# Eight weights of a token-major product prepared ahead, and the MLP's rings in groups of four neighbouring buffers

## The chip, the cores and the metric

The kernel runs on one core of a Trainium2 chip. Its time is the device time of one execution in microseconds (us), lower is better. TensorE (PE) multiplies matrices, with its weight loads shown apart as PEld; VectorE is DVE, ScalarE is ACT, GpSimd is POOL, and SyncE (SP) issues the transfers. Before the change three runs gave 3012.39, 3013.59 and 3018.19 us, a median of 3013.59 us.

## The reference

Two layers, each of three sub-layers on 1024 tokens of width 1024, with a layer norm after each. All is in float32.

```python
def hybrid_mixer(x, positions, w_in, conv_w, rel_bias, w_out):
    proj = jnp.einsum('bsd,dp->bsp', x, w_in)
    (cb, cc, ch, dq, dk, dv, iq, ik, iw, cq, ck, cv) = jnp.split(proj, offs, axis=-1)
    y_conv = short_conv_mixer(cb, cc, ch, conv_w)
    ...                      # partial rope on dq, dk, iq, ik
    y_dsa = dsa_attention(dq, dk, dv, iq, ik, iw)
    y_chk = chunk_band_attention(cq, ck, cv, rel_bias)
    return jnp.einsum('bsm,md->bsd', jnp.concatenate([y_conv, y_dsa, y_chk], -1), w_out)
...
        # in dsa_attention, for each block of 128 queries
        score = jnp.einsum('bqh,bqhs->bqs', iwb, jax.nn.relu(logits))
        _, idx = lax.top_k(score, topk)            # topk = 256
        s = ...                                    # attention on the chosen keys alone
...
for l in range(DEPTH):                             # DEPTH = 2
    x = layer_norm(ALPHA * x + hybrid_mixer(...))
    x = layer_norm(ALPHA * x + memory_cross_attention(x, mem, w_mq, w_mkv, w_mo))
    x = layer_norm(ALPHA * x + squared_relu_mlp(x, w_ff1, w_ff2))   # 1024 -> 4096 -> 1024
```

## The kernel before

Every large product keeps float32 accuracy with rounded operands: an operand is split into a rounded part `hi` and the rest `lo`, and `mm3` (L338) adds three matmuls, hi·hi (L340), hi·lo (L341) and lo·hi (L342). A weight passes through `Weights._emit` (L274): SP moves it to one of four stage buffers (L284), ACT casts it to `hi` (L285), POOL subtracts to get `lo` (L286). `Weights.get(i)` does this for weights up to i + AHEAD, with AHEAD = 4, before the product that uses weight i is written; `prefetch(i)` does it up to weight i where there is room. Both write the instructions at that place in the program. The Tile framework then orders the instructions of each engine by priority and by a simulated timeline, and the engines run their lists in that order. An `Arena` hands out SBUF columns by which of them came free longest ago; a buffer that is taken again makes its new writer wait for the old readers.

Each layer begins with the input projection. Three groups are token-major, by `tok_tile` (L550): the indexer's (key `g1`, weights 128x296), the DSA queries, keys and values (`dsa_proj`, `g2`, 128x512) and the chunk attention's values (`chk_v`, `g3`, 128x384). A group has eight weights, used by all of its eight token tiles, and the first tile of a group asks for its weights one by one with `get`. The chunk queries and keys and the convolution's inputs follow, feature-major. Beside the projections the indexer computes `queries` (L690: rope, a split on POOL L699, a transpose on PE L708), scores each of eight heads on PE (L731), applies the relu on ACT (L736) and sums on DVE (L742 and L744). `topk` (L761) then finds each query's threshold bit by bit, 32 bits: blocks 7 and 6 (group 0) are counted on ACT with Sign (L788), blocks 5 to 2 (group 1) on DVE (L792), and L799 to L811 update the candidate. `masks` (L820) turns thresholds into masks. POOL and DVE also apply the rope (L440 to L443), and L644 (ACT) with L645 (DVE or POOL) is the split of an activation.

`chunk_pair` (L1010) prepares the operands of the chunk attention: ACT scales and rounds the queries (L1022), DVE subtracts (L1023), SP moves halves between partitions (L1019, rows "sb<-sb"); ACT rounds the keys (L1036), POOL subtracts (L1037), and SP moves again. The first scores on PE (L1088) use them. Chunk units and then DSA units follow with their softmax, the weights of the memory products are worked on beside them, and then come the mix output product, the cross attention and its output product.

The MLP is a Strassen product at one level. `up` takes seven products for each of 16 chunks and writes the results `h` to DRAM; the down half takes steps `(p, i)`, p in 5, 7, 3, 1, 4, 6, 2 and i of 16, each of four token tiles with 3 matmuls. `prepare(n)` (L1798) loads an `h` tile and a weight into two `raws` buffers, adds the parts of the weight, and splits both into a `pairs` buffer; DOWN_AHEAD = 7 steps are ahead. `raws` is a ring of 8 buffers of 512 columns, `slots` a ring of kept weights; both are allocated one by one between the two halves.

## Time and profile before

| what | value |
|---|---|
| median of three runs | 3013.59 us |
| profiled execution, its own time | 3010.65 us |
| its span | 3008.8 us |
| PE busy | 2884.2 us, 96% of the span, 14440 matmuls |
| DVE busy | 2155.3 us, 72% |
| ACT busy | 1558.0 us, 52% |
| POOL busy | 1299.5 us, 43% |
| mean DMA rate | 127 GB/s |

The span is that of the one profiled execution, whose own time is 1.85 us longer. PE is the engine that is busy nearly all the time, so the idle time of PE, and the stretches in which PE ran at the lower of its two clock levels, are what can be removed or added without a change of work. In a timeline row the figures are the start, the length of the group of equal instructions, the instruction, and in brackets the idle time of the engine before it with the engine and line that ended it.

### The profile page before, as it was taken

The numbers are of one execution on the slowest core, as the hardware profiler recorded it, in microseconds if no ns is written. First come the engines' busy times: TensorE is split into PE (matmuls) and PEld (weight loads), VectorE is DVE, ScalarE is ACT, GpSimd is POOL, SyncE is SP. The second block draws the span as 40 slices with busy tenths as digits, with TensorE's granted clock in tenths as the row PEclk, the third lists the DMA queues.
The fourth block names the chain that finished last, engine by engine and source line by source line (L and its number), as shares of the span: only waits on it lengthen the run. The fifth ranks groups of instructions, "written<-read, shape, count | busy, mean of one in ns | idle before, by whom it ended". The sixth has DMA issues, their size and how long they took to land. (4 is left out here: it accounts for less than half of the span.)

```text
span 3008.8 us, 43448 instructions
## 1 busy us (share of the span) xinstructions
PE 2884.2 (96%) x14440; PEld 2440.8 (81%) x14440; DVE 2155.3 (72%) x4321; ACT 1558.0 (52%) x3146; POOL 1299.5 (43%) x1242
## 2 busy tenths in 40 slices
PE   8999889999999999999999998899999999999998
PEld 7787778788877788888788877887888778888886
DVE  5897786582487766777857987866625877667788
ACT  5676777623234455543457767784222445554432
POOL 4614575522335553222457146653222555532223
PEclk9999999999999999999999999999999999999999
DMA  4213333331334546755422144232213354476553
GB/s 127 63 36 85 101 110 106 105 119 36 114 116 161 171 154 217 255 178 188 131 68 66 37 100 118 92 117 97 93 47 111 112 175 163 152 250 223 189 179 116
DMA packets 264288, 381.99 MB, mean 127 GB/s; under 512 B 23040, under 2 KB 141824, under 8 KB 264064
## 3 DMA queue, kind: packets, MB, share of 16 engines
q1 hardware_dynamic: 264064, 379.22, 38.7%
q8 instruction: 114, 1.87, 0.3%
q14 instruction: 110, 0.90, 0.1%
HBM read 269.56 MB, written 95.42 MB: 121 GB/s over the span
## 5 line engine op out<-in xcount | busy, mean ns | idle before, releaser
L340 PE MATMUL banks<-sb,sb 128*128 128x512 f32 (+3 forms) x3776 | 1423.0, 378 | 19.7 <-DVE sb L645 6.3
L341 PE MATMUL banks<-sb,sb 128*128 128x512 f32 (+3 forms) x3776 | 1417.7, 376 | 8.6 <-POOL sb L286 8.6
L342 PE MATMUL banks<-sb,sb 128*128 128x512 f32 (+3 forms) x3776 | 1413.9, 376 | 7.7 <-POOL sb L645 7.4
L645 POOL TENSOR_TENSOR sb<-sb,sb 128x512 fp32r<-128x512 f32 (+1 forms) x428 | 590.1, 1390 | 931.3 <-ACT sb L644 793.5
L340 PEld LDWEIGHTS banks<-sb,sb 128*128 128x128 f32 x3776 | 714.3, 189 | 151.4 <-DVE sb L645 9.1
L342 PEld LDWEIGHTS banks<-sb,sb 128*128 128x128 f32 x3776 | 712.7, 189 | 133.2 <-POOL sb L645 9.2
L341 PEld LDWEIGHTS banks<-sb,sb 128*128 128x128 f32 x3776 | 714.4, 189 | 130.8 <-POOL sb L286 10.3
L644 ACT CAST sb<-sb 128x512 fp32r<-128x512 f32 (+1 forms) x788 | 452.8, 605 | 583.5 <-PE banks L341 146.2
L286 POOL TENSOR_TENSOR sb<-sb,sb 128x512 fp32r<-128x512 f32 (+2 forms) x288 | 381.4, 1340 | 480.1 <-ACT sb L285 421.2
L645 DVE TENSOR_TENSOR sb<-sb,sb 128x512 fp32r<-128x512 f32 x360 | 273.2, 785 | 43.8 <-ACT sb L644 41.4
L645 DVE TENSOR_TENSOR sb<-banks,sb 128x384 fp32r<-128x384 f32 (+2 forms) x324 | 188.0, 595 | 86.4 <-ACT sb L644 78.9
L285 ACT CAST sb<-sb 128x512 fp32r<-128x512 f32 (+2 forms) x288 | 170.4, 606 | 136.1 <-PE banks L342 30.4
L644 ACT CAST sb<-banks 128x384 fp32r<-128x384 f32 (+2 forms) x324 | 159.7, 517 | 140.5 <-PE banks L1557 75.3
L792 DVE TENSOR_SCALAR_CACHE_REDUCE sb<-sb,sb 128x768 bf16<-128x768 f32 (+3 forms) x256 | 207.5, 810 | 5.0 <-POOL sb L443 2.0
L1721 DVE TENSOR_TENSOR sb<-sb,sb 128x512 f32<-128x512 f32 x160 | 155.5, 1006 | 60.9 <-ACT sb L1701 56.9
L1005 POOL TENSOR_SCALAR sb<-sb,sb 128x128 f32<-128x128 f32 (+7 forms) x192 | 148.2, 786 | 86.4 <-DVE sb L1003 65.9
L1763 DVE TENSOR_TENSOR sb<-banks,sb 128x512 f32<-128x512 f32 x224 | 149.4, 682 | 47.4 <-PE banks L342 45.7
L788 ACT ACTIVATE sb<-sb,sb 128x1024 bf16<-128x1024 f32 (+1 forms) x128 | 140.4, 1097 | 74.2 <-DVE sb L811 64.9
L1826 DVE TENSOR_TENSOR sb<-sb,sb 128x512 f32<-128x512 f32 x128 | 112.8, 882 | 68.4 <-DMA sb<-w_ff_dram 68.0
L994 ACT ACTIVATE sb<-sb,sb 128x128 f32<-128x128 f32 (+7 forms) x192 | 141.6, 739 | 27.9 <-DVE sb L988 26.5
L1700 ACT ACTIVATE sb<-sb 128x512 f32<-128x512 f32 x128 | 80.7, 631 | 117.6 <-DVE sb L1763 117.1
L1333 DVE SCALAR_TENSOR_TENSOR sb<-sb,banks 128x512 f32<-128x512 f32 x64 | 43.4, 685 | 113.2 <-PE banks L342 110.5
(172 smaller groups left out, 3046.9 us busy)
## 6 DMA issues: line engine op xcount, KB each, us to landing
sb<-h SPq DMA_DIRECT2D x236, 256.0 KB, 3.1
h<-sb SPq DMA_DIRECT2D x224, 256.0 KB, 2.2
sb<-w_ff_dram SPq DMA_DIRECT2D x216, 256.0 KB, 3.1
sb<-w_ff_dram SPq DMA_DIRECT2D x64, 512.0 KB, 4.1
sb<-w_in_dram SPq DMA_DIRECT2D x64, 256.0 KB, 2.9
sb<-w_mkv_dram SPq DMA_DIRECT2D x64, 256.0 KB, 2.8
sb<-sb SPq DMA_DIRECT2D x54, 256.0 KB, 3.6
xs<-sb SPq DMA_DIRECT2D x24, 512.0 KB, 2.8
```

Source lines behind the costliest of these rows:

```text
L285: k.nc.scalar.copy(hi, st)
L286: k.nc.gpsimd.tensor_tensor(lo, st, hi.bitcast(F32), op=ALU.subtract)
L340: mm(out, lh, rh, start=start, stop=False)
L341: mm(out, lh, rl, start=False, stop=False)
L342: mm(out, ll, rh, start=False, stop=stop)
L644: nc.scalar.copy(hi, src)
L645: eng.tensor_tensor(lo, src, hi.bitcast(F32), op=ALU.subtract)
L792: nc.vector.tensor_scalar(junkb[:, :w], x, c, None, op0=ALU.is_ge, op1=ALU.add, accum_out=n)
L994: nc.scalar.activation(pt.ap, pt.ap, AF.Exp, bias=mn, scale=-1.0, accum_out=sm)
L1005: nc.gpsimd.tensor_scalar(pt.ap, pt.ap, rc[:, i : i + 1], 0.0, op0=ALU.mult, op1=ALU.add)
L1721: nc.vector.tensor_tensor(z.ap, x, y, op=ALU.add if spec[1] == "+" else ALU.subtract)
L1763: nc.vector.tensor_tensor(r.ap, ps.ap, part[c, x].ap, op=ALU.add)
```

## The change

Three edits. First, `tok_tile` ends with a `prefetch`: after the tiles t = 4, 5, 6, 7 of a group it asks for the weights up to 2, 4, 6 and 8 behind the group's last one. Since `get` has by then prepared four behind it, the tiles 4 and 5 write nothing new; weights 5 and 6 of the next group are now written behind tile 6, weights 7 and 8 behind tile 7, where they were written in the first tile of the next group. Second, `carve` is built on a new `try_carve`, and the DSA output buffer `st["ys"]` falls back to three buffers where no room for one is left; the number of instructions in the built program shows that the fallback is not taken (32 of the joint add, as before). Third, the MLP takes five groups of four neighbouring 512-column buffers at the top of the arena; the eight `raws` and the first twelve new `slots` come from them.

```diff
     def tok_tile(self, xt, key, l, t, n, last):
...
             if last:
                 self.w.done(wi[k])
+
+        if t >= NT - 4:
+            self.w.prefetch(wi[-1] + 2 * (t - NT + 5))
         return ps
...
-    def carve(self, *cols):
+    def try_carve(self, *cols):
...
-        b = self.alloc(sum(g) * GRAN, top=True)
+        b = self.try_alloc(sum(g) * GRAN, top=True)
+        if b is None:
+            return None
...
-                parts = sb.carve(S, S, S)
-                y = st["ys"] = sb.tensor(parts[0].off, 3 * S, F32)
+                one = sb.try_carve(S, S, S)
+                parts = one or [sb.alloc(S, top=True) for _ in range(3)]
+                st["ys"] = sb.tensor(parts[0].off, 3 * S, F32) if one else None
...
         self.up(l, ops, weights, combos, pend, early())
         ready(0)
         first = len(have)
+
+        fours = [b for _ in range(5) for b in sb.carve(512, 512, 512, 512)]
...
-        raws += [sb.alloc(512) for _ in range(8)]
-        slots += [kept[i] for i in range(first)]
-        slots += [sb.alloc(512) for _ in range(nk + 2 - first)]
+        raws += fours[:8]
+        slots += [kept[i] for i in range(first)] + fours[8:]
+        slots += [sb.alloc(512) for _ in range(nk + 2 - len(slots))]
```

No instruction is added or removed on any engine, but the lists are ordered anew. In the changed kernel the lines are numbered higher: L286 becomes L293, L440 to L443 become L447 to L450, and from L645 on 10 are added (L655, L754, L802, L1032, L1046).

On POOL, in layer 0, the end of the preparation of the `g3` weights (128x384), with the rope of a token tile and the first 128x512 weights of the products that follow. Before:

```order
L286 TENSOR_TENSOR sb_652<-sb_107,sb_652 128x512
L442 TENSOR_TENSOR sb_1047<-sb_1262,sb_794 128x6x8
L443 TENSOR_TENSOR sb_1047<-sb_1262,sb_794 128x6x8
L442 TENSOR_TENSOR sb_1260<-sb_1057,sb_1267 128x8
L443 TENSOR_TENSOR sb_1260<-sb_1057,sb_1267 128x8
L645 TENSOR_TENSOR sb_620<-sb_1260,sb_620 128x64
L286 TENSOR_TENSOR sb_324<-sb_97,sb_324 128x512
L286 TENSOR_TENSOR sb_659<-sb_112,sb_659 128x512
L286 TENSOR_TENSOR sb_1306<-sb_102,sb_1306 128x384
L645 TENSOR_TENSOR sb_577<-sb_1260,sb_577 128x64
```

and now:

```order
L449 TENSOR_TENSOR sb_735<-sb_964,sb_1203 128x6x8
L450 TENSOR_TENSOR sb_735<-sb_964,sb_1203 128x6x8
L449 TENSOR_TENSOR sb_710<-sb_970,sb_1208 128x8
L450 TENSOR_TENSOR sb_710<-sb_970,sb_1208 128x8
L293 TENSOR_TENSOR sb_1264<-sb_107,sb_1264 128x384
L655 TENSOR_TENSOR sb_731<-sb_710,sb_731 128x64
L293 TENSOR_TENSOR sb_310<-sb_97,sb_310 128x512
L293 TENSOR_TENSOR sb_317<-sb_102,sb_317 128x512
L655 TENSOR_TENSOR sb_725<-sb_710,sb_725 128x64
L293 TENSOR_TENSOR sb_1268<-sb_112,sb_1268 128x384
L293 TENSOR_TENSOR sb_324<-sb_107,sb_324 128x512
```

The last 384-wide subtract stood behind three 512-wide ones (before the first of which the other 384-wide ones stand), and now behind two, with the seventh 384-wide one directly ahead of them.

On ACT, in layer 1, the end of the search (Sign, L788, now L798) and the first rounded keys of the chunk attention (the cast L1036, now L1046). Before:

```order
L943 COPY sb_79<-banks 128x512
L788 ACTIVATE sb_901,sb_13627<-sb_12496,sb_13627 128x896
L788 ACTIVATE sb_901,sb_13627<-sb_12498,sb_13627 128x1024
L968 COPY sb_6719<-banks 128x512
L788 ACTIVATE sb_901,sb_13627<-sb_12496,sb_13627 128x896
L644 CAST sb_2817<-sb_3231 128x8x64
L788 ACTIVATE sb_901,sb_13627<-sb_12498,sb_13627 128x1024
L1036 CAST sb_2629<-sb_2748 128x1024
L788 ACTIVATE sb_901,sb_13627<-sb_12496,sb_13627 128x896
L968 COPY sb_905<-banks 128x512
L285 CAST sb_2823<-sb_112 128x512
L644 CAST sb_2825<-sb_3231 128x8x64
```

and now, from the rounded queries (L1032) on:

```order
L1032 ACTIVATE sb_2615<-sb_8191 128x1024
L798 ACTIVATE sb_845,sb_13605<-sb_12496,sb_13605 128x1024
L798 ACTIVATE sb_845,sb_13605<-sb_12494,sb_13605 128x896
L654 CAST sb_2816<-sb_3693 128x8x64
L978 COPY sb_841<-banks 128x512
L1046 CAST sb_2812<-sb_1674 128x1024
L798 ACTIVATE sb_845,sb_13605<-sb_12496,sb_13605 128x1024
L292 CAST sb_1007<-sb_112 128x512
L798 ACTIVATE sb_845,sb_13605<-sb_12494,sb_13605 128x896
L978 COPY sb_837<-banks 128x512
L654 CAST sb_1834<-sb_3693 128x8x64
L798 ACTIVATE sb_845,sb_13605<-sb_12496,sb_13605 128x1024
```

The first cast of the keys had one Sign of the search left behind it in its list, and now has four; the rounded queries had ten behind them and now have six.

On DVE, in layer 1, the sum of the scores (L744, now L754; 128x896 is block 6) and the first counts of the search's group 1 (L792, now L802). Before:

```order
L742 TENSOR_SCALAR sb_12496<-sb_13376,sb_340 128x896
L744 SCALAR_TENSOR_TENSOR sb_12496<-sb_3735,sb_340,sb_12496 128x896
L744 SCALAR_TENSOR_TENSOR sb_12496<-sb_1291,sb_340,sb_12496 128x896
L744 SCALAR_TENSOR_TENSOR sb_12496<-sb_1227,sb_340,sb_12496 128x896
L744 SCALAR_TENSOR_TENSOR sb_12496<-sb_1286,sb_340,sb_12496 128x896
L792 TENSOR_SCALAR sb_4486,sb_13627<-sb_12494,sb_13627 128x768
L744 SCALAR_TENSOR_TENSOR sb_12496<-sb_13443,sb_340,sb_12496 128x896
L792 TENSOR_SCALAR sb_4486,sb_13627<-sb_12492,sb_13627 128x640
L744 SCALAR_TENSOR_TENSOR sb_12496<-sb_5154,sb_340,sb_12496 128x896
L792 TENSOR_SCALAR sb_4486,sb_13627<-sb_12490,sb_13627 128x512
L744 SCALAR_TENSOR_TENSOR sb_12496<-sb_13452,sb_340,sb_12496 128x896
L742 TENSOR_SCALAR sb_12498<-sb_135,sb_340 128x1024
```

and now:

```order
L754 SCALAR_TENSOR_TENSOR sb_12492<-sb_3459,sb_340,sb_12492 128x768
L752 TENSOR_SCALAR sb_12494<-sb_1227,sb_340 128x896
L802 TENSOR_SCALAR sb_899,sb_13605<-sb_12492,sb_13605 128x768
L802 TENSOR_SCALAR sb_899,sb_13605<-sb_12490,sb_13605 128x640
L802 TENSOR_SCALAR sb_899,sb_13605<-sb_12488,sb_13605 128x512
L754 SCALAR_TENSOR_TENSOR sb_12494<-sb_13366,sb_340,sb_12494 128x896
L802 TENSOR_SCALAR sb_899,sb_13605<-sb_12486,sb_13605 128x384
L814 TENSOR_SCALAR sb_13605<-sb_13605 128x4
L819 TENSOR_SCALAR sb_13605<-sb_13605 128x4
L802 TENSOR_SCALAR sb_899,sb_13605<-sb_12492,sb_13605 128x768
L754 SCALAR_TENSOR_TENSOR sb_12494<-sb_3739,sb_340,sb_12494 128x896
L802 TENSOR_SCALAR sb_899,sb_13605<-sb_12490,sb_13605 128x640
```

The first counts stood behind four of the 896-wide sums, between further sums, and now stand ahead of all but the first instruction of that block.

## Rows read from the trace of the kernel before

**Rows 1.** Page of the profile: span, then busy time and instructions of each engine.

```profile
span 3008.8 us, 43448 instructions
...
PE 2884.2 (96%) x14440; PEld 2440.8 (81%) x14440; DVE 2155.3 (72%) x4321; ACT 1558.0 (52%) x3146; POOL 1299.5 (43%) x1242
```

**Rows 2.** Windows: start and end, length, busy time by engine, clock, DMA share, GB/s.

```profile
113.00:155.00 42.00, 37.79 (x193) 33.86 (x192) 41.56 (x71) 26.46 (x55) 19.61 (x25) 0.96 0.34 89
...
126.30:129.70 3.40, 3.14 (x10) 2.33 (x9) 3.40 (x6) 1.52 (x3) 0.51 (x2) 0.50 0.50 128
...
1050.00:1425.00 375.00, 375.00 (x1657) 310.59 (x1655) 271.17 (x374) 182.83 (x315) 130.94 (x93) 1.00 0.58 199
...
1590.00:1613.00 23.00, 23.00 (x117) 20.12 (x116) 11.42 (x11) 16.14 (x34) 17.60 (x33) 1.00 0.14 40
...
2525.00:2925.00 400.00, 400.00 (x1766) 331.21 (x1765) 292.95 (x404) 195.56 (x337) 141.63 (x100) 1.00 0.58 197
```

**Rows 3.** Waits of PE, one kind: total us, times, longest.

```profile
PE banks L341 <- POOL sb L286: 8.6, 4, 2.5
```

**Rows 4.** PE's timeline, layer 0: start, length, instruction, idle before and releaser.

```profile
106.86 0.88 PE L708 MATMUL banks<-sb,sb 128*128 128x128 f32 x8 [1.28 <-POOL sb L699]
...
125.59 0.45 PE L341 MATMUL banks<-sb,sb 128*128 128x384 f32 x1 [2.54 <-POOL sb L286]
...
296.17 6.72 PE L1088 MATMUL banks<-sb,sb 128*128 128x128 f32 x18 [4.89 <-DMA sb<-sb]
```

**Rows 5.** PE's timeline, layer 1.

```profile
1615.00 0.44 PE L341 MATMUL banks<-sb,sb 128*128 128x384 f32 x1 [1.59 <-POOL sb L286]
...
1618.90 0.45 PE L341 MATMUL banks<-sb,sb 128*128 128x384 f32 x1 [2.19 <-POOL sb L286]
...
1785.06 3.61 PE L1088 MATMUL banks<-sb,sb 128*128 128x128 f32 x10 [2.21 <-DMA sb<-sb]
```

**Rows 6.** POOL's timeline, layer 0 and layer 1.

```profile
121.25 4.29 POOL L286 TENSOR_TENSOR sb<-sb,sb 128x512 fp32r<-128x512 f32 x3
...
1604.37 1.02 POOL L286 TENSOR_TENSOR sb<-sb,sb 128x384 fp32r<-128x384 f32 x1
...
1613.94 4.90 POOL L286 TENSOR_TENSOR sb<-sb,sb 128x384 fp32r<-128x384 f32 x3
```

**Rows 7.** ACT's timeline, end of the search, layer 0 and layer 1.

```profile
280.93 1.15 ACT L788 ACTIVATE sb<-sb,sb 128x1024 bf16<-128x1024 f32 x1 [0.61 <-DVE sb L811]
...
282.08 1.04 ACT L1022 ACTIVATE sb<-sb 128x1024 fp32r<-128x1024 f32 x1
...
285.04 1.05 ACT L1036 CAST sb<-sb 128x1024 fp32r<-128x1024 f32 x1
...
1751.63 1.06 ACT L1022 ACTIVATE sb<-sb 128x1024 fp32r<-128x1024 f32 x1
...
1773.11 1.04 ACT L1036 CAST sb<-sb 128x1024 fp32r<-128x1024 f32 x1
```

**Rows 8.** VectorE's timeline, the search in layer 0 and layer 1.

```profile
106.19 1.10 DVE L742 TENSOR_SCALAR sb<-sb,sb 128x896 f32<-128x896 f32 x1 [1.35 <-ACT sb L736]
...
115.83 1.16 DVE L744 SCALAR_TENSOR_TENSOR sb<-sb,sb,sb 128x896 f32<-128x896 f32 x1
...
121.23 2.25 DVE L744 SCALAR_TENSOR_TENSOR sb<-sb,sb,sb 128x896 f32<-128x896 f32 x1
...
1645.27 0.15 DVE L811 SCALAR_TENSOR_TENSOR sb<-sb 128x2 int32<-128x2 int32 x1
...
1649.11 0.15 DVE L811 SCALAR_TENSOR_TENSOR sb<-sb 128x2 int32<-128x2 int32 x1
```

**Rows 9.** Page of the profile: two groups of instructions (busy us, mean ns), one DMA issue.

```profile
L645 POOL TENSOR_TENSOR sb<-sb,sb 128x512 fp32r<-128x512 f32 (+1 forms) x428 | 590.1, 1390 | 931.3 <-ACT sb L644 793.5
...
L644 ACT CAST sb<-sb 128x512 fp32r<-128x512 f32 (+1 forms) x788 | 452.8, 605 | 583.5 <-PE banks L341 146.2
...
sb<-h SPq DMA_DIRECT2D x236, 256.0 KB, 3.1
```

More of the change, by code (lines that the diff above doesn't have):

```diff
@@ L161, in carve @@
         return res
+    def carve(self, *cols):
+        b = self.try_carve(*cols)
+        assert b is not None, ("SBUF is full", cols, self.room())
+        return b
     def room(self):
@@ L1258, in values @@
             if b == 0 and hg == 0:
-                parts = sb.carve(S, S, S)
-                y = st["ys"] = sb.tensor(parts[0].off, 3 * S, F32)
+                one = sb.try_carve(S, S, S)
+                parts = one or [sb.alloc(S, top=True) for _ in range(3)]
+                st["ys"] = sb.tensor(parts[0].off, 3 * S, F32) if one else None
                 for f, x in enumerate(parts):
-                    st["y"][2 + f] = Part(x, y[:, f * S : (f + 1) * S])
-            y = st["ys"]
-            nc.vector.tensor_tensor(
-                y.rearrange("p (f s) -> p f s", f=3)[
-                    hg * HD : (hg + 1) * HD, :, b * P : (b + 1) * P
-                ],
-                po.ap[0:HD, 0:384].rearrange("p (f s) -> p f s", f=3),
-                low.ap[0:HD, :].rearrange("p (f s) -> p f s", f=3), op=ALU.add,
-            )
+                    y = st["ys"][:, f * S : (f + 1) * S] if one else x.ap
+                    st["y"][2 + f] = Part(x, y)
+            rows, q = slice(hg * HD, (hg + 1) * HD), slice(b * P, (b + 1) * P)
+            if st["ys"] is not None:
+                nc.vector.tensor_tensor(
+                    st["ys"].rearrange("p (f s) -> p f s", f=3)[rows, :, q],
+                    po.ap[0:HD, 0:384].rearrange("p (f s) -> p f s", f=3),
+                    low.ap[0:HD, :].rearrange("p (f s) -> p f s", f=3), op=ALU.add,
+                )
+            else:
+                for f in range(3):
+                    c = slice(f * P, (f + 1) * P)
+                    nc.vector.tensor_tensor(
+                        st["y"][2 + f].ap[rows, q], po.ap[0:HD, c], low.ap[0:HD, c],
+                        op=ALU.add,
+                    )
             self.ps.free(po)
```

## The prediction

> **What bounds the kernel now.** I read the page first. PE is busy 2884.2 of 3008.8 us [rows 1], so no other engine bounds the kernel as a whole, and an edit that adds and removes no instruction can only move three things: PE's idle time (3008.8 - 2884.2 = 124.6 us), the stretches at PE's lower clock level, and what ends PE's waits. Next I took the windows by stage. In both MLPs PE is busy 375.00 of 375 and 400.00 of 400 us at a granted clock of 1.00 [rows 2]: nothing is to be gained there, and what matters is how much room stands before PE starts to wait. Third, the table of PE's waits by kind shows what the change aims at, the third product of a token tile waiting for the weight's `lo` part from POOL: 8.6 us in 4 waits [rows 3]. Fourth, PE's timeline shows where. One of the waits is in layer 0 (2.54 us at 125.59), two are in layer 1 (1.59 at 1615.00, 2.19 at 1618.90) [rows 4, 5], together 6.3 us; the fourth, 8.6 - 6.3 = 2.3 us, is in another product that the change doesn't touch. Last I followed both layers to the point where the projections give way to the first chunk scores. There PE waits for the moves between partitions, 4.89 us at 296.17 and 2.21 us at 1785.06 [rows 4, 5]. That is the important thing to see: a stall that is removed earlier in the same layer brings PE sooner to a wait that a different chain ends, that of the search on ACT and DVE, the operands behind it, and their moves.
>
> **The edits that cost nothing.** The new `carve` and its fallback issue the same instructions. The MLP's rings lie elsewhere, so a load may wait for the last reader of other columns; the first four `raws` now lie where an operand of the second-last up product was. The cover is PE's queue. A matmul takes 375.00/1657 = 0.226 us there [rows 2]; the up product still to run after that one has 12 matmuls (2.7 us), and the first four steps of the down half, prepared earlier, have 4 x 12 (10.9 us), together 13.6 us. A step prepared in a new buffer needs a load of 3.1 us, a cast of 0.605 and a split of 1.39, and the cast and split again for the second operand at most, 3.1 + 2 x 2.0 = 7.1 us [rows 9]. So the rings cost 0, and if the cover were gone it would be up to 7.1 us once per layer.
>
> **The prefetch in layer 0.** It can remove the wait at 125.59: 2.54 us, and with it the low clock that follows. From 126.3 to 129.7 PE was busy 3.14 us at a granted clock of 0.50 (1.2 GHz), after the engine had stood still; at the full level the same work takes half, 1.6 us less [rows 2, 4]. That makes 4.1 us for PE. How sure is it? In the order the last 384-wide subtract on POOL still stands behind two 512-wide ones, where it stood behind three; three subtracts together took 4.29 us [rows 6], so it may come about 1.4 us sooner, besides what the earlier load gives. The bounds of the stall itself are 0 and 4.1.
>
> How much of it reaches the first scores is set by the other chain. Their operands move as follows: in the new list of ACT the rounded queries (L1022) stand one Sign earlier, ahead of that at 280.93, which began after 0.61 us of waiting and took 1.15 [rows 7]. So they, and the moves behind them, may come 0.61 + 1.15 = 1.76 us earlier at the same pace of the search. The search itself may begin earlier: at 106.86 PE waits 1.28 us for the queries' split on POOL, and just before, at 106.19, DVE had stood still 1.35 us for the relu [rows 4, 8]; in POOL's new list this split stands ahead of a rope. I count 1.0 of the 1.28. Layer 0 so gives 1.8 + 1.0 = 2.8 us; its bounds are 0 and 4.1 + 1.3 = 5.4.
>
> The subtracts are moved beside the dense part of the search, and there they have a price. DVE is busy 41.56 of 42 us from 113 to 155 [rows 2], so whatever slows it there moves the search as a whole. A sum of block 6 took 1.16 us at 115.83 and 2.25 us at 121.23, where POOL's three subtracts ran [rows 6, 8]. They ran in the dense part before, too, so I count no new cost. The Trainium skill ("SBUF — State Buffer", section "Who interferes with whom") says that DVE and GpSimd share one pair of ports under an exclusive lock; by this rule two more subtracts there would take from DVE up to 2 x (2.25 - 1.16) = 2.2 us, and layer 0 would give 2.8 - 2.2 = 0.6 instead of 2.8. The trace agrees that a sum beside the subtracts is slower, 2.25 against 1.16 us, and not that the whole of it is new.
>
> **The prefetch in layer 1.** The two stalls are 1.59 + 2.19, and a third of 0.5 us follows them in the same place, together 4.3 us at the full clock. POOL made three 384-wide subtracts in 4.90 us there, where one alone took 1.02 [rows 6]: its late `lo` parts are partly DVE's doing. Against this stands the other chain, which now runs in another order. First gain: the first cast of the keys stands behind 60 Signs, not 63 (before, at 1773.11 [rows 7]), so its operands can come earlier than 1773.11 at an equal pace. First loss: the rounded queries stand behind 58, not 54 (before, at 1751.63), yet 1751.63 lies far ahead of the keys and sets nothing. The pace is the open term. The scores' products of the last block come later in the new program, and group 1's search ends with four bits of group 0 left, not two. Near the end of group 1 a bit takes 1649.11 - 1645.27 = 3.84 us [rows 8]. If group 1's search starts no earlier, the end of group 0 comes two bits later, 7.7 us. It can start earlier: its first counts stand ahead of the 896-wide sums now, and from 1590 to 1613 DVE is busy only 11.42 of 23 us, 11.6 us idle [rows 2]. So layer 1 lies between -7.7 and +4.3. I take 2.5, nearer to the upper end, because the idle 11.6 us are more than the 7.7 that they must cover, and less than 4.3, because PE's 2.21 us of waiting at 1785.06 shows that the operands are late already.
>
> **The attention units** are ordered anew in both layers, with no instruction more or less. Some of PE's 124.6 idle us lie there, behind splits and softmax steps on DVE, and a new order can lose or gain; no row says which, so I count 0. As the nearest measure for both ends I take the waits of rows 4 and 5 that are not on weights, 4.89 + 2.21 + 1.28 = 8.4 us [rows 4, 5].
>
> **The sum.** 2.8 + 2.5 = 5.3 us, against the profiled execution 3010.65 - 5.3 = 3005.3. The median of the runs stands 2.9 us above that execution, so in medians 3013.6 - 5.3 = 3008.3, which I give as 3008.
>
> **The rivals.** A difference of 0.2%, 6 us, is about what a measurement of this kernel can tell from none.
>
> A, the forecast, 3008, chance 0.50. Its own range is 3013.6 - 9.7 = 3004 (both layers at their upper bound, 5.4 + 4.3) to 3011 (half of the sum), and it is faster by over 0.2% in about half of these cases: 0.24 faster, 0.25 same, 0.01 slower.
>
> B, absorbed: PE comes earlier to the first scores and waits longer there, or POOL's last subtract of `g3`, still behind two wide ones, is hardly sooner. For it speaks the 4.89 us wait at 296.17, larger than all that is removed before it; against it that the operands, too, stand earlier in ACT's lists of both layers. What is left is the 1.0 of the queries' split: 3012.6. Chance 0.17: 0.02, 0.13, 0.02.
>
> C, slower: in layer 1 the search starts no earlier and ends two bits later, so masks and the DSA scores behind them come 7.7 us later, and the counts and Signs run on into the attention, where they stand ahead of the softmax on DVE and ACT. It decides if group 1's first count does not come at least 7.7 us sooner than the sums allow now. The price is 7.7: 3021. For it speaks that three subtracts and the rope stand beside DVE there, and that the last block's score products come later in the new lists; against it the 11.6 idle us before. Chance 0.18: 0, 0.01, 0.17.
>
> D, faster: the stalls go, and the new order of the attention units also takes out some 6 to 7 of the waits there, 5.3 + 6.7 = 12, or 3001.6, say 3001. For it speaks that these waits are short and follow single late splits; against it that nothing in the edits aims at them. Chance 0.15, all faster.
>
> Together: faster 0.24 + 0.02 + 0.15 = 0.41, same 0.25 + 0.13 + 0.01 = 0.39, slower 0.01 + 0.02 + 0.17 = 0.20. The range reaches from 2996, where the upper bounds of both layers meet an attention better by 8, to 3021, where C stands.
>
> **What the profile afterwards would show.** The first step is right if no wait of L341 (now L348) for POOL's subtract is left near 125 and 1615, and if the clock is 1.00 after 126. The second is right if PE waits at the first chunk scores no longer than 4.89 + (5.4 - 2.8) = 7.5 and 2.21 + (4.3 - 2.5) = 4.0 us; if these grow by all that went before, it is B. Rival C shows as a last Sign of layer 1 that ends later against the end of the projections, with the first counts no earlier. The MLP windows must still show PE busy all the time; a wait of the products for a load of `h` would make the zero for the rings wrong. The prediction as a whole is wrong if the difference lies outside of the attention and projection stages.

## The result and the profile after

The changed kernel is slower. Four runs gave 3026.74 to 3032.12 us, median 3029.9; the ratio to the kernel before (now four runs, median 3013.8) is 1.0057 [1.0045, 1.0069], 0.6% or some 17 us. Its profiled execution took 3026.74 us (span 3025.0), 16.2 us of span more than the one of before.

The page, for [rows 1] (span; busy time by engine):

```profile
span 3025.0 us, 43421 instructions
...
PE 2895.5 (96%) x14440; PEld 2449.3 (81%) x14440; DVE 2161.7 (71%) x4321; ACT 1558.4 (52%) x3146; POOL 1292.2 (43%) x1242
```

PE is busy 11.3 us longer with the same 14440 matmuls: the same work went at a lower clock. To see where, I cut both executions at places that both have, the first transposes behind a layer norm: of layer 0's mix norm, of layer 0's end, of layer 1's mix norm. The last of the four stretches ends with the last matmul, 15 us before the span's end. These are windows (start and end, length, busy time of PE, PEld, DVE, ACT, POOL, mean clock, DMA share, GB/s), first before:

```profile
0.00:628.20 628.20, 579.33 (x3251) 503.37 (x3252) 470.69 (x1227) 411.19 (x896) 310.92 (x373) 0.97 0.30 90
628.20:1453.10 824.90, 813.07 (x3755) 675.63 (x3753) 566.65 (x867) 353.48 (x655) 317.23 (x242) 1.00 0.47 158
1453.10:2117.30 664.20, 624.74 (x3452) 540.73 (x3453) 502.60 (x1276) 423.24 (x916) 333.86 (x375) 0.97 0.30 90
2117.30:2994.00 876.70, 867.05 (x3985) 721.04 (x3983) 604.25 (x938) 368.81 (x678) 335.12 (x251) 0.99 0.45 153
```

and after:

```profile
0.00:622.60 622.60, 576.73 (x3260) 500.70 (x3261) 470.63 (x1226) 412.64 (x896) 309.82 (x373) 0.99 0.31 91
622.60:1447.50 824.90, 812.45 (x3747) 675.29 (x3745) 557.45 (x866) 353.77 (x656) 320.21 (x244) 0.99 0.47 158
1447.50:2126.70 679.20, 635.72 (x3452) 550.54 (x3453) 517.09 (x1277) 422.44 (x917) 325.44 (x374) 0.95 0.29 88
2126.70:3010.00 883.30, 870.55 (x3985) 722.78 (x3983) 605.46 (x937) 368.32 (x678) 334.43 (x251) 0.99 0.45 152
```

Layer 0's projections and attention gain 5.6 us, its rest nothing. Layer 1's projections and attention lose 15.0: 4.0 of idle PE (679.20 - 635.72 against 664.20 - 624.74) and 11.0 of longer PE time for as many matmuls. The last stretch loses 6.6. Sum: -5.6 + 15.0 + 6.6 = 16.0. The first chunk scores of layer 1 divide its 15.0 once more: they came 337.7 us behind the layer's first transpose, before 332.0, and from them to the stretch's end it is 341.5 us, before 332.2. So 5.7 are lost ahead of them and 9.3 behind.

The waits that the change aimed at are gone, as [rows 3] to [rows 5] after show (PE's waits by kind; then PE's timeline, with the idle time before and its releaser):

```profile
PE banks L348 <- POOL sb L293: 0.5, 1, 0.5
```

```profile
146.86 0.69 PE L347 MATMUL banks<-sb,sb 128*128 128x384 f32 x1 [5.59 <-ACT sb L927]
...
295.26 7.11 PE L1098 MATMUL banks<-sb,sb 128*128 128x128 f32 x20 [3.63 <-ACT sb L978]
...
1785.22 5.21 PE L1098 MATMUL banks<-sb,sb 128*128 128x128 f32 x14 [3.31 <-DMA sb<-sb]
...
1907.78 1.43 PE L1098 MATMUL banks<-sb,sb 128*128 128x320 f32 x4 [2.08 <-DVE sb L998]
...
2716.63 0.71 PE L347 MATMUL banks<-sb,sb 128*128 128x512 f32 x1 [3.64 <-ACT sb L654]
```

8.6 us in four waits became 0.5 in one. In layer 0 another wait stands a little later in their place: at 146.86 PE waits 5.59 us for a bank, whose copies (L927) stood in ACT's list behind a Sign that waited for the last block's scores. The first scores came only 0.9 us sooner in layer 0 (296.17, now 295.26) and no sooner in layer 1 (1785.06, now 1785.22), although layer 1 began 5.6 us earlier. Two more places stand out, and windows show them:

```profile
1893.00:1917.00 24.00, 19.69 (x130) 17.50 (x128) 23.94 (x47) 11.81 (x28) 13.34 (x12) 0.81 0.14 42
1907.80:1924.90 17.10, 14.16 (x63) 12.33 (x64) 14.71 (x35) 12.02 (x30) 14.44 (x12) 0.50 0.30 88
...
2700.00:2725.00 25.00, 21.36 (x88) 17.19 (x87) 11.58 (x17) 15.32 (x28) 3.87 (x3) 0.93 1.04 398
```

The first is in layer 1's attention: DVE has no free moment from 1893 to 1917, PE waits, and the clock is 0.50 (1.2 GHz) for 17.1 us. DVE's timeline tells what it does there:

```profile
1897.16 2.02 DVE L876 TENSOR_TENSOR_SCAN sb<-sb 128x896 f32<-128x896 f32 x1
...
1903.88 2.27 DVE L876 TENSOR_TENSOR_SCAN sb<-sb 128x1024 f32<-128x1024 f32 x1
...
1906.08 1.12 DVE L877 SCALAR_TENSOR_TENSOR sb<-sb,sb,sb 128x896 f32<-128x896 f32 x1
1907.12 0.15 DVE L1013 RECIPROCAL sb<-sb 128x2 f32<-128x2 f32 x1
1907.19 0.53 DVE L998 CUSTOM_DVE_ANT_0 sb<-banks,sb,sb 128x320 f32<-128x320 f32 x1
```

These are parts of the masks of the last two blocks, 6 (896 wide) and 7 (1024), at once; the softmax minimum (L998) for which PE waits stands behind them. In DVE's list the two masks end behind 134 and 138 softmax instructions of layer 1, before the change behind 128 and 176. The second place is the start of layer 1's down half, where the DMA engines are full (share 1.04) and PE waits for a step's split.

### The profile page after: what moved, and what is told of

It reads as the page before. It is cut to its first block, busy times and chain, and to the rows that moved or that the text cites. A ratio compares the mean times of both kernels' runs of the same rounds, so it can differ in the third digit from the quotient of the medians.

```text
span 3025.0 us, 43421 instructions
## 1 busy us (share of the span) xinstructions
PE 2895.5 (96%) x14440; PEld 2449.3 (81%) x14440; DVE 2161.7 (71%) x4321; ACT 1558.4 (52%) x3146; POOL 1292.2 (43%) x1242
## 5 line engine op out<-in xcount | busy, mean ns | idle before, releaser
L347 PE MATMUL banks<-sb,sb 128*128 128x512 f32 (+3 forms) x3776 | 1422.4, 379 | 33.6 <-ACT sb L654 10.0
L348 PE MATMUL banks<-sb,sb 128*128 128x512 f32 (+3 forms) x3776 | 1419.3, 376 | 0.7 <-POOL sb L293 0.5
L655 POOL TENSOR_TENSOR sb<-sb,sb 128x512 fp32r<-128x512 f32 (+1 forms) x428 | 592.1, 1395 | 933.5 <-ACT sb L654 814.3
L347 PEld LDWEIGHTS banks<-sb,sb 128*128 128x128 f32 x3776 | 715.8, 190 | 167.8 <-ACT sb L654 12.8
L348 PEld LDWEIGHTS banks<-sb,sb 128*128 128x128 f32 x3776 | 716.2, 190 | 122.0 <-POOL sb L293 0.9
L293 POOL TENSOR_TENSOR sb<-sb,sb 128x512 fp32r<-128x512 f32 (+2 forms) x288 | 379.0, 1331 | 477.9 <-ACT sb L292 388.3
L655 DVE TENSOR_TENSOR sb<-sb,sb 128x512 fp32r<-128x512 f32 x360 | 290.2, 834 | 39.7 <-ACT sb L654 38.9
L655 DVE TENSOR_TENSOR sb<-banks,sb 128x384 fp32r<-128x384 f32 (+2 forms) x324 | 185.7, 595 | 69.2 <-ACT sb L654 67.7
L802 DVE TENSOR_SCALAR_CACHE_REDUCE sb<-sb,sb 128x768 bf16<-128x768 f32 (+3 forms) x256 | 207.6, 811 | 6.4 <-POOL sb L759 3.5
L1740 DVE TENSOR_TENSOR sb<-sb,sb 128x512 f32<-128x512 f32 x160 | 155.7, 1008 | 69.7 <-ACT sb L1720 65.6
L1015 POOL TENSOR_SCALAR sb<-sb,sb 128x128 f32<-128x128 f32 (+7 forms) x192 | 141.3, 751 | 120.7 <-DVE sb L1013 88.3
L798 ACT ACTIVATE sb<-sb,sb 128x1024 bf16<-128x1024 f32 (+1 forms) x128 | 140.3, 1096 | 59.9 <-DVE sb L821 52.0
L1845 DVE TENSOR_TENSOR sb<-sb,sb 128x512 f32<-128x512 f32 x128 | 100.5, 785 | 70.1 <-DMA sb<-w_ff_dram 69.6
L998 DVE CUSTOM_DVE_ANT_0 sb<-banks,sb 128x128 f32<-128x128 f32 (+5 forms) x192 | 96.3, 509 | 46.3 <-PE banks L1098 18.6
```

What stands on the lines that cost most here:

```text
L293: k.nc.gpsimd.tensor_tensor(lo, st, hi.bitcast(F32), op=ALU.subtract)
L347: mm(out, lh, rh, start=start, stop=False)
L348: mm(out, lh, rl, start=False, stop=False)
L655: eng.tensor_tensor(lo, src, hi.bitcast(F32), op=ALU.subtract)
L802: nc.vector.tensor_scalar(junkb[:, :w], x, c, None, op0=ALU.is_ge, op1=ALU.add, accum_out=n)
L1015: nc.gpsimd.tensor_scalar(pt.ap, pt.ap, rc[:, i : i + 1], 0.0, op0=ALU.mult, op1=ALU.add)
```

## The experiments

Theory 1: three costs, each at its place (two masks in a row in layer 1's attention; layer 1's prefetch, by a later search; the rings, by a burst of loads), against a gain in layer 0. Theory 2: the rings cost nothing, all is the prefetch. Theory 3: each edit draws the lists anew, and nothing adds up. Beside the ratio of the runs I give the lengths of the four stretches above, from each kernel's profile. The kernel before ran again beside every group of runs, with medians from 3013.8 to 3017.1 us, so ratios are to be compared, not times. A stretch comes from one execution, and executions of equal lists differ: the first scores of layer 0 came at 295.3 and at 300.3 us in two kernels with equal lists there, the ten kernels with the prefetch in layer 0 have equal lists in stretch 1 and took 621.5 to 630.3 us for it, and r1 and r2, whose lists are those of e2 and of the changed kernel throughout, differ from these by up to 5.3 us in a stretch.

| kernel | ratio to before, 95% | stretch 1 | 2 | 3 | 4 |
|---|---|---|---|---|---|
| before | 1 | 628.2 | 824.9 | 664.2 | 876.6 |
| after | 1.0057 [1.0045, 1.0069] | 622.6 | 824.9 | 679.2 | 883.4 |
| e2 rings only | 1.0035 [1.0021, 1.0050] | 630.1 | 834.6 | 666.0 | 878.2 |
| e3 prefetch layer 0, rings | 0.9969 [0.9958, 0.9980] | 624.0 | 825.3 | 665.3 | 878.2 |
| e4 prefetch layer 1, rings | 1.0047 [1.0035, 1.0059] | 628.2 | 831.9 | 671.4 | 882.9 |
| e8 prefetch layer 1, no rings | 1.0060 [1.0042, 1.0079] | 627.0 | 825.6 | 672.7 | 881.1 |
| n1 FILL 180 | 0.9982 [0.9972, 0.9993] | 631.6 | 825.7 | 666.3 | 875.7 |
| m1 mask 7 later | 1.0029 [1.0016, 1.0042] | 624.2 | 826.6 | 670.7 | 883.3 |
| k1 masks side by side | 1.0023 [1.0008, 1.0038] | 630.3 | 829.3 | 665.1 | 885.6 |
| f1 filler later | 0.9982 [0.9973, 0.9991] | 621.5 | 825.5 | 675.8 | 870.0 |
| r1 rings, x written later | 1.0036 [1.0022, 1.0049] | 628.2 | 830.6 | 665.7 | 879.5 |
| r2 after, x written later | 1.0067 [1.0051, 1.0084] | 627.9 | 827.1 | 677.4 | 883.5 |
| g1 rings, x gated | 1.0023 [1.0012, 1.0034] | 629.2 | 826.4 | 671.0 | 880.3 |
| g3 after, x gated | 1.0022 [1.0010, 1.0034] | 624.0 | 825.9 | 678.0 | 879.8 |
| m2 mask 7 later, x gated | 1.0015 [1.0002, 1.0028] | 624.2 | 826.5 | 668.8 | 887.4 |
| b1 all of it in layer 0 alone | 0.9982 [0.9972, 0.9992] | 626.5 | 826.8 | 663.8 | 876.2 |
| g2 e3, x gated | 0.9992 [0.9982, 1.0002] | 627.8 | 825.0 | 662.9 | 880.3 |

### The parts alone

**e2**, the prefetch taken out:

```diff
-        if t >= NT - 4:
-            self.w.prefetch(wi[-1] + 2 * (t - NT + 5))
```

> The change without the prefetch: the rings in fours alone. Theory 1 (the prefetch in layer 1 costs some 15 us there, the rings some 7 us in layer 1's MLP, and the prefetch gives back 5.6 us in layer 0): 3014 + 7 = 3021, and the wait near the start of layer 1's down half stays. Theory 2 (the rings cost nothing, all of it is the prefetch): 3014. Theory 3 (the scheduler's order is a new draw with any edit, so the parts don't add): neither, anywhere within 15 us of 3014.

Measured 3026.28 us, 1.0035. Theory 2 falls: the rings alone cost, and they cost in layer 0's MLP (834.6 against 824.9). Theory 1 forecast 3021 with the cost in layer 1's down half; in e2 PE has no such wait there. In layer 1 the table of waits has no L348 behind POOL's subtract at the `g3` weights, without any prefetch: the two stalls there went with the new order that the rings bring. Its first scores in layer 1 came 330.7 us behind the first transpose, 1.3 sooner than before (r1 2.3 sooner, g1 1.9 later): without the stalls, and hardly sooner.

**e3**, the prefetch in layer 0 alone:

```diff
-        if t >= NT - 4:
+        if t >= NT - 4 and l == 0:
```

> Rings and the prefetch in layer 0 alone. Its lists are those of the changed kernel until layer 1's projections. Theory 1: the gain of 5.6 us in layer 0 stays and the loss of 15 us in layer 1 goes, so about 3030 - 15 = 3015. Theory 2: the same 3014 - 5.6 = 3008. Theory 3: layer 1 lies anywhere, as much as 15 us from either.

Measured 3008.58 us, 0.9969: faster than both kernels, and by its ratio (9 us below before) lower than theory 1's 3015 and theory 2's 3008 beside 3014. Against the changed kernel layer 1's last stretch lost its 5 us as well.

**e4**, the same with `l == 1`.

> Rings and the prefetch in layer 1 alone. Theory 1: layer 1's loss of 15 us stays, layer 0's gain goes: 3014 + 15 + 7 = 3036. Theory 3: layer 1 has other lists than in the changed kernel, since the emission before differs, and its loss is not 15.

Measured 3031.19 us, 1.0047. Layer 1 loses 7 us in stretch 3 and 6 in stretch 4, layer 0 has the rings' cost as in e2. In stretch 3 that is smaller than 15: the pair of masks isn't in its list (132 and 174). Theory 1's 3036 was too high.

**e8**, the kernel before with the prefetch at `l == 1`, rings as before.

> The kernel before with the prefetch in layer 1 alone, without the rings: the one part that meets the stalls of 1.6 and 2.2 us that it was predicted to remove there. Layer 0 is word for word that of before. The prediction's own step: 2.5 us faster, 3011 to 3015 beside a before of 3014 to 3017. Theory 1 (in layer 1 the prefetch costs, since the scores' sums and with them the search of the last two blocks come later): 6 to 15 us slower. No mask stands next to another in its list of DVE, so of theory 1 the part with the masks is not in it: then 5 us slower at most.

Measured 3031.38 us, 1.0060, more than any theory said (2.5 us faster, 5 or 6 to 15 slower). The stalls in layer 1 are gone, and the 2.5 us that they were to give don't come: its first scores stand 332.4 us behind the first transpose, before 332.0. Stretch 3 is 8.5 us longer, nearly all of it idle PE behind the first scores (340.3 against 332.2; one window, as above):

```profile
1452.60:2125.30 672.70, 625.01 (x3453) 541.97 (x3454) 506.23 (x1308) 423.65 (x916) 329.63 (x375) 0.97 0.30 89
```

672.70 - 625.01 = 47.7 us of idle time against 39.5 before. But e8 is not the prefetch alone. In its layer 1 no room was left for the one DSA output buffer, so that the fallback to three buffers was taken: 48 joint adds (L1286) stand where 16 stood, 13.3 us of DVE for 8.8. k1 below took it, too, and its attention lost nothing (331.8 us behind the first scores). So what the loss in e8 comes from stays open; and the profile is of the fastest of its six runs, 8 us below their median.

**n1**, one number of the kernel before: `FILL = 180` for 200.

> The kernel before with one number changed that neither part of the change touches: FILL, the priority of the memory products beside the attention, 180 for 200. It aims at nothing. Theory 1: within 6 us of 3014, since neither prefetch nor rings are there. Theory 3: it moves by as much as the change, 6 to 16 us in either direction, because the attention's lists are drawn anew.

Measured 3012.41 us, 0.9982. Smaller than the effects here, but not nothing: an edit that aims at nothing moved the time by 0.2%. Its lists differ from those of before only from 1848 us on, in layer 1's attention, so it is a small sample of a new order. It moves less than the 0.8 to 0.9% between e3 and the changed kernel, e4 and e8; but k1 below, one number away from e3, moved by 0.5%. Theory 3 so holds in part, and a difference in time alone shows no cause.

### The masks in layer 1

**m1**, the changed kernel with the last mask written later:

```diff
-                yield 7.5
+                yield 9.0 if b == 6 and st["layer"] == 1 else 7.5
```

> The changed kernel with one number more: in layer 1 the step after the mask of block 6 counts 9 for 7.5, so that the last mask (block 7) is written a little later. In DVE's list it then stands behind 178 softmax instructions of the attention where the changed kernel has it behind 138, next to the mask of block 6 (behind 134, now 130). Theory 1 (two masks of 896 and 1024 columns in a row hold DVE, PE waits for the softmax there and falls to the lower clock for 17 us): the low clock around 1908 goes, 8 to 10 us less, 3020 to 3022. Theory 3 (the loss in layer 1 is spread over the stage and has no one place): within 4 us of 3030. Rival (the late end of the search holds the attention): 3030, since the search ends as before.

Measured 3022.88 us, 1.0029, 0.28% or some 8 us less than the changed kernel, and stretch 3 is 8.5 us shorter. In the 17 us in which DVE was held the clock is 1.00:

```profile
1907.00:1924.00 17.00, 13.33 (x101) 11.56 (x100) 10.79 (x38) 14.82 (x42) 14.22 (x19) 1.00 0.32 92
```

The search ended 336.3 us after layer 1's first transpose, in the changed kernel 335.9, before 324.2. Behind the first scores m1's attention took 332.3 us, as before (332.2), and not 341.5: the late search as such doesn't slow the attention. It does make it begin late: the first scores stand 338.4 us behind the first transpose, before 332.0, and that is all by which m1's stretch 3 is still longer. The same lists up to there gave 337.2 to 338.5 us in six kernels (the changed one, m1, f1, r2, g3, m2).

**k1**, e3 with the same line and 5.0.

> The kernel with rings and the prefetch in layer 0 alone (0.9969 of before), and in layer 1 the step after the mask of block 6 counts 5 for 7.5. DVE's list is the same up to there; the last mask then stands behind 138 softmax instructions, next to block 6's (132), where it stood behind 170, as in the changed kernel. Nothing of the prefetch in layer 1 is in it and its search ends as before. Theory 1 (two masks in a row hold DVE and drop PE's clock, whatever brought them together): the attention stage of layer 1 takes 8 to 10 us more, 3017 to 3019. Rival (the late search, or the new order as a whole, cost the time in the changed kernel): 3008.6 within 4.

Measured 3027.01 us, 1.0023, slower than e3, but not at the place that theory 1 said: stretch 3 stayed (665.1) and stretch 4 grew by 7 with a wait of 3.95 us at 2715.40, the burst below. Behind the first scores it took 331.8 us. Two masks in a row alone do not cost in the attention; the rival was right there, but both times, its 3008.6 and theory 1's 3017 to 3019, were too low. k1 took the fallback of e8 in layer 1, too, its runs fall into two groups (3018 to 3019 and 3027 to 3029), and its profile, of the upper group, is 10 us longer than e3's in stretches 1 and 2, where the lists are equal. So its time says little.

**f1**, the changed kernel with the memory products, which fill PE beside the attention, begun later in layer 1:

```diff
-                    self.after(START, RATE, self.shift(FILL, self.memory(l, st))),
+                    self.after(START if l == 0 else 34, RATE, ...
```

> The changed kernel with the memory products of layer 1 begun 4 steps later beside the attention (34 for 30), so that they also end later. The last two masks still stand side by side in DVE's list (behind 130 and 138 softmax instructions). In the changed kernel the memory products, which fill PE between the attention's dependent matmuls, end some 120 us after the first scores, and the two masks end at 123 and 131; in the kernel with masks side by side that lost nothing in this stage they end at 117 and 125. If the loss needs both, masks in a row and no fillers left: the 17 us of low clock go or halve, 5 to 9 us less, 3021 to 3025. If the masks in a row are enough: 3030 as before.

Measured 3011.72 us, 0.9982, 0.75% or some 23 us less than the changed kernel, by one number. The theory had 5 to 9, so the place that it names is at most a part of that. Windows of the first of the three products (L347) alone, 100 to 140 us behind the first scores (length, busy PE and PEld, clock, DMA share, GB/s), first of the changed kernel:

```profile
1885.00:1905.00 20.00, 9.25 (x32) 6.09 (x32) 1.00 0.32 103
1905.00:1925.00 20.00, 0.79 (x2) 0.62 (x2) 0.57 0.26 76
```

then of f1:

```profile
1884.00:1904.00 20.00, 5.84 (x18) 3.83 (x18) 0.91 0.16 54
1904.00:1924.00 20.00, 6.62 (x20) 3.80 (x20) 0.91 0.30 96
```

The masks still stand side by side. PE has 20 of these matmuls where it had 2, and the clock is 0.91, not 0.57. So the loss needs both, masks in a row and no filler left; in k1 the last instructions of the two masks began 116.5 and 125.3 us after the first scores, in the changed kernel 123.4 and 130.8. The filler ended 119 us after them in the changed kernel, so ahead of both, and at 127.5 in k1. That the few us between them decide was not tried by itself. f1's stretches 3 and 4 together are 16.8 us shorter than the changed kernel's. 38 matmuls of 128x512 went from stretch 4 to stretch 3 (3490 for 3452); at 0.227 us each, the distance of their starts at full clock, they are 8.6 us, an estimate. So some 12 are gained in stretch 3 and 5 in stretch 4, where the new lists have no wait at the down half any more, which the edit didn't aim at.

Together: the three profiles with two masks in a row and no filler (the changed kernel, r2, g3) took 341.5, 338.9 and 340.0 us behind the first scores and have 17.1, 13.7 and 17.1 us of low clock at the masks; m1, m2 and f1 (less the 8.6) took 332.3, 330.9 and 330.0, and have no stretch of over 6.8 us near theirs.

### The burst of loads at the down half

**r1** and **r2**, rings only and the changed kernel, with the residual's eight loads written at i = 9, 11, 13, 15 for 6, 8, 10, 12.

> Rings alone, with the loads of the residual (eight of 512 KB) written three steps later in the down half. Theory 1 (in the rings' layout these loads find their buffers free sooner and fill the DMA engines just before the first steps' loads of h and weights, so that PE waits 5.2 us in layer 0 and runs at the lower clock for 6.8 us after it): the wait near the start of layer 0's down half goes, 7 to 9 us less than rings alone. Rival (PE waits because the ring buffers' own earlier readers are late): the wait stays, no difference beyond 3 us.

> The changed kernel with the same later loads of the residual. Theory 1: the 3.6 us wait at the start of layer 1's down half goes with its low clock, 5 us less, 3025. Rival as in the run before: no difference beyond 3 us.

Measured 3025.98 (1.0036) and 3033.48 us (1.0067). Inconclusive: the lists of all engines came out as without the edit, so it moved nothing. They serve as repeats of e2 and of the changed kernel.

**g1**, rings only with a gate:

```diff
+                nc.vector.tensor_copy(xs[t].ap[:, 0:1], have[n][0].r[:, 0:1].bitcast(F32))
                 nc.sync.dma_start(xs[t].ap, self.x2[t * P : (t + 1) * P, :])
```

> Rings alone, and before each load of the residual in the down half one column of its buffer is written by DVE from the operand of the step in whose turn it is written, so that the load starts after that step's own h and weight have landed (16 small DVE instructions more). In SP's list the eight loads move from rows 436 to 459 to rows 454 to 503. The two runs with later-written loads left them where they were, so that the question of the DMA burst is still open; this one moves them. Theory 1 (burst of the residual's loads ahead of the first steps' loads): the wait of 3.6 to 5.2 us at the start of layer 0's down half goes with the low clock behind it, and the stretch from layer 0's mix norm to layer 1's first transpose falls from 831 to 835 to 825 to 827; in time 5 to 8 us less than rings alone. Rival: the wait stays and the time with it.

Measured 3022.77 us, 1.0023, 0.12% less than e2, with intervals that overlap, and stretch 2 826.4 against 834.6 and 830.6. The start of layer 0's down half in e2, PE's timeline and a window (its L651 is L644 of the kernel before):

```profile
1219.02 0.80 PE L347 MATMUL banks<-sb,sb 128*128 128x512 f32 x1 [5.15 <-ACT sb L651]
```

```profile
1195.00:1225.00 30.00, 24.85 (x98) 20.03 (x97) 14.66 (x18) 17.34 (x32) 7.87 (x7) 0.89 1.02 376
```

and the same start in g1:

```profile
1190.00:1240.00 50.00, 50.00 (x223) 41.40 (x222) 30.19 (x45) 31.56 (x58) 15.16 (x12) 1.00 0.89 312
```

The wait is gone. In e2 seven loads of the residual were issued within 20 us among the steps' own, in g1 two. The stage gained, the time hardly (5 to 8 were expected): stretches 3 and 4 were drawn anew, and 3 came out longer.

**g3**, the changed kernel with the gate.

> The changed kernel with the residual's loads gated: each waits for the operands of the step in whose turn it is written (16 small DVE instructions more). If the burst of these loads is what costs the last stage of the changed kernel (3.6 us of waiting at the start of layer 1's down half and the low clock behind it), that stage falls from 832 to 826 to 828 and the time by 4 to 6 us, to about 3025. If the last stage is late for other reasons, the wait goes and the stage stays at 830 or more, within 3 us of 3030.

Measured 3021.32 us, 1.0022, 0.35% or some 10 us less, where 4 to 6 were expected. In the profile the wait at the start of layer 1's down half is gone and stretch 4 is 3.6 us shorter; the pair of masks and its 17.1 us of low clock are still there. The rest of the 10 us has no place in the profile, whose matmuls end only 2.3 us sooner.

**m2**, both repairs.

> The changed kernel with both repairs, the later last mask and the gated loads. If the two costs add: 3023 (the later mask alone) less 4 to 6, 3017 to 3019. What is then left against before (some 3 us) are layer 1's projections, which end later, less layer 0's gain. If they don't add, 3023.

Measured 3019.97 us, 1.0015, 0.14% less than m1, with intervals that overlap, so whether the two add isn't shown: the runs lie from 3011 to 3030, and in the profiled one a wait of 4.25 us came up among the last products (at 2944.36, for the variance's square root on DVE).

**b1**, prefetch and rings in layer 0 alone, and **g2**, e3 with the gate.

> Both parts of the change in layer 0 alone: prefetch there, rings there, layer 1's down half as before the change. Expected as the version without rings in layer 1, where they cost 1 to 2 us: 3006 to 3009, 0.996 to 0.997 of before. If the rings of layer 1 are what makes its last stage what it is, more than 5 us either way.

> Rings in both layers, the prefetch in layer 0 alone, and the residual's loads gated as in the first of these runs. Its down halves show no wait for the burst, so theory 1 expects no gain from the gate and at most 1 us for the 16 instructions: 3008 to 3010.

Measured 3011.29 us (0.9982) and 3012.71 us (0.9992). b1's stretches 3 and 4 are those of before, so the rings in layer 1 are not what makes e3 fast; the gate gains nothing where no burst was. Both stand some us above e3, about the size of n1. b1's lists are those of e3 until the down half of layer 1, and the intervals of the two overlap: they are hardly told apart. The lowest ratio is e3's, 0.9969, faster than both kernels.

## Why the prediction was wrong, step by step

It forecast 3008 and a range to 3021; the time is 3029.9. The terms were -2.8 in layer 0, -2.5 in layer 1 and 0 for the attention and the rings; the profile has -5.6, +5.7 ahead of layer 1's first scores, +9.3 behind them, and +6.6 in the last stretch.

- **Layer 0's stall** (1.8 + 1.0 us). It went, and the first scores gained 0.9: a new wait of 5.6 us for L927 took its place, with 3.4 us at a clock of 0.50 behind it (146.5 to 149.9), as long as behind the old one. The rounded queries came 1.0 us sooner, but the search began only 0.5 sooner (first Sign at 145.1, before 145.6). Yet stretch 1 gains: the ten kernels with the prefetch in layer 0 took 621.5 to 630.3 us, mean 625.3, the seven without it 627.0 to 631.6, mean 628.9, so 3.6 us. Of these 0.7 lie ahead of the first scores and 2.9 behind them (means of the same kernels), and in the changed kernel the mean clock of the stretch rose from 0.97 to 0.99. The size, 2.8, was right by luck: the way was another, and why the attention has less low clock there isn't settled.
- **Layer 1's stalls** (2.5 us, "because the idle 11.6 us are more than the 7.7 that they must cover"). This is the step that failed: the first scores came not 2.5 us sooner but 5.7 later. The 11.6 idle us of [rows 2] were no room for the search. Nearly all of them are DVE's sums waiting for ACT's relu of the scores (waits of DVE from 1590 to 1613, before):

```profile
DVE sb L744 <- ACT sb L736: 10.5, 4, 3.7
```

  The score products themselves went back: in the changed kernel PE's last one stands behind 899 matmuls of the layer, before behind 855, and began 184.0 us after the first transpose, before 172.9. The first counts of group 1 came earlier, as forecast (1606.36, before 1613.42), but group 0 decides, which needs the last block's scores, and it began later: its first Sign at 1640.29 against 1637.97, in a layer that began 5.6 us sooner (192.8 and 184.9 us behind the first transpose). The search's last update (the kind of [rows 8]) came at 1783.37, before at 1777.26. The keys' cast, three Signs earlier in the list, came 3 us later in time (ACT's timeline, first Sign before and after, then the cast, for [rows 7]):

```profile
1637.97 1.16 ACT L788 ACTIVATE sb<-sb,sb 128x1024 bf16<-128x1024 f32 x1 [1.26 <-POOL sb L749]
...
1640.29 1.15 ACT L798 ACTIVATE sb<-sb,sb 128x1024 bf16<-128x1024 f32 x1 [0.62 <-POOL sb L759]
...
1776.03 1.04 ACT L1046 CAST sb<-sb 128x1024 fp32r<-128x1024 f32 x1
```

  A place in a list says what a thing stands behind, not when that comes. In all 17 profiles layer 1's first scores came 144 to 147 us after its first Sign. The prediction's sign for this step, a wait of at most 4.0 us at the first scores, was met (3.31) and didn't show the failure: over the whole way to it PE stood idle 2.9 us longer and was busy 2.8 us longer with as many matmuls. About half of the 5.7 stands in e3 as well, whose layer 1 has no prefetch (334.6), so not all of it is the prefetch there.
- **Rival C** named the mechanism: a later search in layer 1. By its own condition it held, since the first count came 7.1 us sooner and not 7.7. It had a chance of 0.18 and the price 7.7, taken one for one from two bits of the search. The size was near, 5.7 in the changed kernel and 5.2 to 6.5 in the six with its lists; but it was paid ahead of the first scores, and the counts and Signs that run on into the attention, which C named, cost nothing there (m1).
- **The rings at 0.** Wrong in part. Their cover was worked out for one step that is prepared late; nothing was said of what else is issued there. Loads of 512 KB come close together and fill the DMA engines: in e2 seven were issued within 11 us, before five within 6 us and three more 17 us later. The stage is 6 to 10 us longer in layer 0 of e2, e4 and r1, and some 4 in layer 1 of the changed kernel (g3). The gate shows that PE's wait hangs on these loads. They are not enough by themselves: in the changed kernel's layer 0 eight were issued within 17 us, in f1's layer 1 within 18, and PE did not wait. What else it takes isn't settled. [Rows 2] show PE busy throughout at a DMA share of 0.58, but that is a mean over some 400 us. At the start of layer 1's down half the engines were full in the kernel before, too, and PE was busy throughout:

```profile
2690.00:2700.00 10.00, 10.00 (x45) 8.26 (x45) 9.47 (x14) 8.72 (x17) 2.58 (x2) 1.00 1.04 407
```

- **The attention's new order at 0, with 8.4 us on both sides.** Mis-sized: 9.3 us in layer 1 alone (6.7 and 7.8 in r2 and g3, whose lists there have the same pair of masks). What cost is the pair of masks where PE had no filler left, and the clock that fell with it (m1, f1).
- **What remains open.** In e8 and e4 layer 1's stretch 4 is 4 to 6 us longer; e4 has a wait of 2.76 us at its down half (2718.2), e8, without the rings, has none. Of the changed kernel's 6.6 us there the gate took back 3.6. Why the score products went back in PE's list is the scheduler's, and no run changed that alone. e8's idle time has no one place. The kernels without two masks in a row took 326.6 to 340.3 us behind layer 1's first scores, so other new orders are worth as much as the pair of masks.

## What to carry to other kernels

Where a scheduler orders the work, an edit that writes loads earlier is an edit of every list behind it: here the stall that it aimed at went, and part of the price was paid where two engines' queues meet, some 300 us later. Idle time of an engine is no room for other work until it is known what the engine waits for. Before promising a gain, find the chain that ends the next wait (here from the first Sign to the first scores, some 145 us) and ask whether the edit moves its start. Before trusting such an edit look in the new lists for two long instructions that come to stand next to each other on a busy engine, and ask whether the bottleneck has filler left beside them; here one start number of the filler brought the ratio from 1.0057 to 0.9982, though more than that place changed by it. Test the parts per layer, since the same edit gained in one layer and lost in the other; look whether a part still issues the same instructions, as e8 and k1 did not; and run more than one edit that aims at nothing to learn how much a new order alone is worth.

## What the runs showed of the hardware

A kernel's time rose by the clock more than by waiting: in layer 1's stretch 3 idle time grew by 4.0 us, and PE's time for the same 3452 matmuls by 11.0. At 1907.8 a wait of 2.08 us behind a stretch of dependent matmuls went over into 17.1 us at 0.50, in which PE was busy 14.16 us. And a transfer of 256 KB took 5.9 us to land beside the residual's 512 KB loads at a share of 1.0 (median of ten loads of `h` in the changed kernel from 2690 to 2720), where its median over the whole kernel before is 3.1 us [rows 9]. In the kernel before it took 5.6 us at the same place (13 loads from 2675 to 2712, share 1.00).
